# The last store of an AdaLoRA forward kernel: two rows per partition taken out of it and sent in nineteen small transfers

## The chip, the cores and the metric

The kernel runs on one core of a Trainium2 chip. A core has five engines that run at the same time: TensorE (PE) for matrix products, VectorE (DVE), ScalarE (ACT), GpSimd (POOL) and SyncE (SP). Each works through its own list of instructions in order, and they wait for each other by semaphores. Sixteen DMA engines move data between the chip's memory (HBM) and the core's own memory (SBUF, 128 partitions). A transfer is issued by an instruction of one of the engines; from then on the DMA engines do the work, and when it has landed its semaphore has risen by 16.

The metric is the time of one execution on the device in microseconds (us). Lower is better.

## The reference

`x` is 16 x 2048 rows of 256 numbers, all float32, `W` is 256 x 256, `lora_A` is 256 x 16, `lora_B` is 16 x 256, `lora_E` has 16 numbers and `scale` is 1.0.

```python
x_flat = x.reshape(-1, in_dim)                 # 32768 x 256
y = x_flat @ W
lora_out = x_flat @ lora_A
lora_out = lora_out * lora_E
lora_out = lora_out @ lora_B
y = y + scale * lora_out
return y.reshape(batch, seq_len, out_dim).astype(np.float32)
```

33.6 MB of `x` have to come in and 33.6 MB of `y` have to go out.

## The kernel before

The small matrices are folded into one at the start: `weff = W + scale * A * E * B` in bfloat16 (lines 149 to 156 and 224 to 233, and TensorE's lines 277 to 287). After that the kernel is one product of `x` with `weff`.

The 32768 rows are cut into 32 steps of 1024 rows (`S` = 8 rows in each of 128 partitions). Steps are grouped into chunks by `PLAN`: ten chunks of three steps and a last one of two. A chunk is what one load or one store moves: 24 rows of 1 KB per partition, 3 MB, or in the last chunk 16 rows per partition, 2 MB. `rows_of` (line 114) gives a chunk's rows in HBM, and a partition's rows lie there one behind the other; `rows_at` (line 118) gives them in SBUF. The tensor `xy` holds four buffers of 24 rows, and `X_AT` and `Y_AT` say which buffer a chunk of `x` or of `y` uses.

Each step goes through the engines like this. VectorE rounds its rows to bfloat16 (`xb`, line 198). TensorE transposes them (line 258), ScalarE or VectorE copies the transposed rows to `xt` (line 188), which keeps 22 steps, VectorE moves a step to `xm` (line 211), TensorE multiplies it with `weff` in two halves (line 267), and ScalarE or VectorE copies each half from PSUM to the buffer of `y` (line 180). The order of VectorE's work is written out in `VECTOR`, and TensorE's comes from `FIRST` and `SECOND`.

All transfers are issued by SP, in this order: `w_sb`, the first chunk of `x`, `a_sb`, `b_sb`, `e_sb`, the other ten loads, and then the eleven stores. A load whose buffer is in use waits for the transposes that read it (line 128). A store waits until both halves of its last step have been copied (semaphores `s_rdy`, line 140), and the first store also waits for the last load but one (line 143). Loads and stores of chunk `i` share the semaphore `s_io[i]`: 16 once `x` has landed, 32 once `y` has.

After the last store has been issued, SP waits for the first eight stores (line 146), which closes the first block of the program. A second block at the end (lines 298 to 300) waits for the last three stores. It shows in the profile under line 331, where the program is closed.

GpSimd makes the identity matrix and `b_bf`, and then it only passes on semaphores (lines 159 to 164). It issues no transfers.

Of the kernel before, what the change touches and what calls it, by code (L numbers as in the profile page):

```python
# [9 lines left out]
S, Q = 8, 4  # L10

PLAN = [3] * 10 + [2]
# [4 lines left out]
Y_AT = [3, 1, 2, 0, 3, 1, 2, 0, 3, 1, 2]  # L17

KEPT = 22


FIRST = [6, 7, *range(14, 28)]
# [12 lines left out]
def kernel(  # L35
# [10 lines left out]
    nc = tc.nc  # L46
    P = 128
# [4 lines left out]
    out_flat = out.flatten_outer_dims()  # L52
# [4 lines left out]
    H = S // Q  # L57
    CHUNKS, STEPS = len(PLAN), sum(PLAN)
# [4 lines left out]
    def sbuf(name, shape, dt):  # L63
        return ctx.enter_context(nc.sbuf_tensor(name, shape, dt))
# [7 lines left out]

    xt = sbuf("xt", [P, KEPT, S, P, KC], BF16)
    xm = [sbuf(f"xm{s}", [P, S, P, KC], BF16) for s in range(2)]
# [15 lines left out]
    sem = tc.alloc_semaphore  # L90
    s_w = sem("s_w")
    s_l = sem("s_l")
    s_io = [sem(f"s_io{i}") for i in range(CHUNKS)]
    s_id = sem("s_id")
    s_lora = sem("s_lora")
    s_lpe = sem("s_lpe")
# [7 lines left out]
    s_rdy = [sem(f"s_rdy{h}") for h in range(H)]  # L104
# [9 lines left out]
    def rows_of(flat, i):  # L114
        r0, n = first[i] * S * P, PLAN[i] * S
        return flat[r0:r0 + n * P, :].rearrange("(p b) k -> p b k", b=n)

    def rows_at(buffer, r, rows):
        return xy[:, at[buffer] * S + r:at[buffer] * S + r + rows, :]

    with tc.tile_critical(sync_engine=mybir.EngineType.SP, no_gpsimd_drain=True):  # L121
        sp, pe, dve, act, pool = nc.sync, nc.tensor, nc.vector, nc.scalar, nc.gpsimd
# [15 lines left out]
        for i in range(CHUNKS):  # L138
            for h in range(H):
                sp.wait_ge(s_rdy[h], i + 1)  # L140
            if i == 0:

                sp.wait_ge(s_io[CHUNKS - 2], 16)
            sp.dma_start(out=rows_of(out_flat, i), in_=rows_at(Y_AT[i], 0, PLAN[i] * S)).then_inc(s_io[i], 16)
        for i in range(CHUNKS - 3):
            sp.wait_ge(s_io[i], 32)

# [4 lines left out]
            out=ident[:], in_=ident[:], compare_op=mybir.AluOpType.not_equal, fill=1.0,  # L152
# [6 lines left out]
        for k in range(STEPS):  # L159
            pool.wait_ge(s_mv, k + 1).then_inc(s_m, 1)  # L160
            i = chunk[k] - 1
            if k > 0 and i >= 0 and k == first[i + 1]:
                for h in range(H):
                    pool.wait_ge(s_rdy[h], i + 1).then_inc(s_y[h], 1)


        known = {}

        def ensure(engine, semaphore, value):
            if known.get((engine, semaphore.name), 0) < value:  # L170
                engine.wait_ge(semaphore, value)
                known[engine, semaphore.name] = value
# [11 lines left out]
        def transposes_of(k, engine, copy):  # L184
            ensure(engine, s_t, k + 1)
            if k >= KEPT:
                ensure(engine, s_mv, k - KEPT + 1)
            copy(  # L188
                out=xt[:, k % KEPT].rearrange("w j p c -> w j (p c)"), in_=ps_xt[k % 2][:].bitcast(BF16),
            ).then_inc(s_c[k % 2], 1)  # L190
# [11 lines left out]
        def move(k):  # L202
# [6 lines left out]
            if k >= 2:  # L209
                ensure(dve, s_p, (k - 1) * H)  # L210
            dve.tensor_copy(out=xm[k % 2][:], in_=xt[:, k % KEPT]).then_inc(s_mv, 1)  # L211

        vectors = set(VECTOR.split())
        for what in VECTOR.split():
            n = int(what[1:])
# [8 lines left out]
            if what == "r0":  # L224
# [3 lines left out]
                    out=ate[:], in0=ps_at, scalar1=e_sb[:], scalar2=float(scale),  # L228
# [69 lines left out]
    with tc.tile_critical(sync_engine=mybir.EngineType.SP, no_gpsimd_drain=True):  # L298
        for i in range(CHUNKS - 3, CHUNKS):
            nc.sync.wait_ge(s_io[i], 32)  # L300


# [33 lines left out]
```

## Time and profile before

| What | Value |
|---|---|
| time, median of 2 runs | 166.28 us (166.25 to 166.31) |
| time of the profiled execution | 166.21 us |
| its span, from the first to the last instruction | 164.4 us |
| TensorE busy | 103.4 us (63%) |
| VectorE busy | 99.9 us (61%) |
| ScalarE busy | 72.1 us (44%) |
| GpSimd busy | 1.6 us (1%) |
| moved by DMA | 67.43 MB, mean 410 GB/s over the span |
| last store (2 MB), from issue to landing | 13.7 us |

The profile counts times from the first instruction of the span. Its page cuts the span into 40 equal slices, here of 4.1 us, and gives one digit for each: 9 means busy for 90% or more. The row "DMA" is the mean over the 16 DMA engines. In the list of waits each line names the waiting engine and line, what it waited for, the total in us, the number of times, and the longest; a small q behind an engine's name means its sequencer. A line of the timeline has start, duration, engine, source line, operation and the names written and read.

### The profile page before, as it was taken

How to read it: one execution, taken by the hardware profiler on the slowest of the kernel's cores; microseconds unless marked ns; L12 is line 12 of the kernel's file. 1: busy time of each engine (PE TensorE's matmuls, PEld its weight loads, DVE VectorE, ACT ScalarE, POOL GpSimd, SP SyncE). 2: the span in 40 equal slices, each digit the busy share in tenths (PEclk: the TensorE clock that was granted, in tenths of full speed). 3: DMA queues.
4: the chain of work that ended last, by engine and by line, in shares of the span. 5: the costliest groups of instructions: out<-in, count | busy, mean ns of one | idle time of the engine just before them, and what ended most of it. 6: DMA issues, size and time to landing. Idle time of an engine off the chain costs nothing. (4 is left out here: it accounts for less than half of the span.)

```text
span 164.4 us, 2431 instructions
## 1 busy us (share of the span) xinstructions
PE 103.4 (63%) x772; PEld 82.0 (50%) x772; DVE 99.9 (61%) x101; ACT 72.1 (44%) x62; POOL 1.6 (1%) x7
## 2 busy tenths in 40 slices
PE   0003763858884567966799887878878787880000
PEld 0001652747674447745699665655666565560000
DVE  0016699786969496787999765667466466730000
ACT  3000254146796413441477665446546544652000
POOL 1002000000000000000000000000000000000000
PEclk9999999599999675599999999999999999999555
DMA  5999999999999999999999999999999999999970
GB/s 165 460 403 460 401 460 401 460 401 460 401 466 395 466 395 466 395 466 385 420 460 401 454 407 460 413 442 424 436 424 436 424 432 424 442 424 430 426 301 12
DMA packets 3523, 67.43 MB, mean 410 GB/s; under 512 B 560, under 2 KB 576, under 8 KB 704
## 3 DMA queue, kind: packets, MB, share of 16 engines
q1 hardware_dynamic: 3520, 67.41, 96.2%
q14 instruction: 3, 0.02, 0.0%
HBM read 33.85 MB, written 33.55 MB: 410 GB/s over the span
## 5 line engine op out<-in xcount | busy, mean ns | idle before, releaser
L267 PE MATMUL ps_y<-weff,xm 128*128 128x256 bf16 x512 | 62.8, 272 | 9.9 <-PEq L264 8.8
L180 ACT COPY xy<-ps_y 128x1024 f32<-128x1024 f32 x49 | 48.7, 1016 | 35.2 <-PE ps_y L267 34.5
L267 PEld LDWEIGHTS ps_y<-weff,xm 128*128 128x128 bf16 x512 | 47.3, 97 | 24.3 <-issue 19.2
L258 PE MATMUL ps_xt<-ident,xb 128*128 128x128 f32 x256 | 41.4, 319 | 21.9 <-PEq L256 21.8
L198 DVE CAST xb<-xy 128x2048 bf16<-128x2048 f32 x32 | 38.6, 1221 | 23.7 <-DMA xy<-in_x_dram 20.2
L258 PEld LDWEIGHTS ps_xt<-ident,xb 128*128 128x128 f32 x256 | 34.7, 165 | 28.2 <-issue 28.1
L188 ACT COPY xt<-ps_xt 128x2048 bf16<-128x2048 bf16 x12 | 22.4, 1868 | 41.1 <-PE ps_xt L258 41.1
L180 DVE COPY xy<-ps_y 128x1024 f32<-128x1024 f32 x15 | 18.4, 1225 | 17.2 <-PE ps_y L267 17.2
L188 DVE COPY xt<-ps_xt 128x2048 bf16<-128x2048 bf16 x20 | 24.2, 1216 | 1.0 <-PE ps_xt L258 0.9
L211 DVE COPY xm<-xt 128x2048 bf16<-128x2048 bf16 x32 | 21.8, 685 | 4.4 <-PE ps_y L267 4.4
L280 PE MATMUL ps_y<-ident,a_sb 128*16 128x128 f32 x2 | 0.6, 402 | 12.2 <-DMA e_sb<-in_lora_E_dram 12.2
L280 PEld LDWEIGHTS ps_y<-ident,a_sb 128*16 128x16 f32 x2 | 0.1, 94 | 12.2 <-DMA e_sb<-in_lora_E_dram 12.2
L188 ACT ACT_TABLE_LOAD x1 | 1.3, 1283 | 0.9 <-SPq L121 0.9
L233 DVE TENSOR_TENSOR weff<-w_sb,ps_y 128x512 bf16<-128x512 f32 x1 | 0.7, 687 | 0.8 <-PE ps_y L284 0.8
L156 POOL CAST b_bf<-b_sb 16x256 bf16<-16x256 f32 x1 | 0.9, 912 | 10.6 <-DMA e_sb<-in_lora_E_dram 10.6
L284 PE MATMUL ps_y<-b_bf,ate 16*128 16x256 bf16 x2 | 0.6, 404 | 0.6 <-DVE ate L227 0.6
L284 PEld LDWEIGHTS ps_y<-b_bf,ate 16*128 16x128 bf16 x2 | 0.1, 106 | 1.1 <-DVE ate L227 1.1
L227 DVE TENSOR_SCALAR ate<-ps_y,e_sb 16x256 bf16<-16x256 f32 x1 | 0.5, 472 | 0.0
L151 POOL TENSOR_SCALAR_AFFINE_SELECT ident<-ident 128x128 f32<-128x128 f32 x1 | 0.3, 294 | 0.2 <-POOL ident L149 0.2
L149 POOL MEMSET ident<- 128x128 f32 x1 | 0.2, 205 | 0.5 <-SPq L121 0.5
L317 POOL MEMSET const-bfloat16-1.0<- 128x1 bf16 x1 | 0.1, 103 | 0.0
L317 POOL MEMSET const-uint8-127<- 128x1 uint8 x1 | 0.1, 102 | 0.0
(2 smaller groups left out, 0.2 us busy)
## 6 DMA issues: line engine op xcount, KB each, us to landing
xy<-in_x_dram SPq DMA_DIRECT2D x10, 3072.0 KB, 14.4
out_dram<-xy SPq DMA_DIRECT2D x10, 3072.0 KB, 12.5
xy<-in_x_dram SPq DMA_DIRECT2D x1, 2048.0 KB, 12.7
out_dram<-xy SPq DMA_DIRECT2D x1, 2048.0 KB, 13.7
w_sb<-in_W_dram SPq DMA_DIRECT2D x1, 256.0 KB, 2.7
a_sb<-in_lora_A_dram SPq DMA_DIRECT2D x1, 16.0 KB, 9.4
b_sb<-in_lora_B_dram SPq DMA_DIRECT2D x1, 16.0 KB, 9.2
e_sb<-in_lora_E_dram SPq DMA_DIRECT2D x1, 0.1 KB, 9.4
```

What stands on the lines that cost most here:

```text
L151: pool.affine_select(out=ident[:], in_=ident[:], compare_op=mybir.AluOpType.not_equal, fill=1.0, base=0, pattern=[[-1, P]], channel_multip ...
L156: pool.tensor_copy(out=b_bf[:], in_=b_sb[:]).then_inc(s_lora, 1)
L180: done = copy(out=rows_at(Y_AT[i], (k - first[i]) * S + h * Q, Q), in_=ps_y[h][:])
L188: copy(out=xt[:, k % KEPT].rearrange("w j p c -> w j (p c)"), in_=ps_xt[k % 2][:].bitcast(BF16),).then_inc(s_c[k % 2], 1)
L198: dve.tensor_copy(out=xb[k % 2][:], in_=rows_at(X_AT[i], (k - first[i]) * S, S),).then_inc(s_xb, 1)
L211: dve.tensor_copy(out=xm[k % 2][:], in_=xt[:, k % KEPT]).then_inc(s_mv, 1)
L227: dve.tensor_scalar(out=ate[:], in0=ps_at, scalar1=e_sb[:], scalar2=float(scale), op0=mybir.AluOpType.mult, op1=mybir.AluOpType.mult,).the ...
L233: dve.tensor_add(out=weff[:], in0=w_sb[:], in1=ps_aeb).then_inc(s_lora, 1)
L258: t = pe.transpose(ps_xt[b][:, j, :], xb[b][:, j, :].bitcast(FP32), ident[:])
L267: m = pe.matmul(ps_y[h][:, j, :], xm[b][:, h * Q + j, :, c], weff[:, c, :], start=(c == 0), stop=(c == KC - 1),)
L280: t = pe.transpose(ps_at[:, c, :], a_sb[:, c, :], ident[:])
L284: m = pe.matmul(ps_aeb[:, c, :], ate[:, c, :], b_bf[:], start=True, stop=True)
```

## The change

The last store, that of chunk 10, no longer covers all 16 rows of each partition. It moves the first 14, in one transfer as before. Row 15 of the 128 partitions follows in sixteen transfers on SP's queue: the first takes 15 partitions, the next 14, and so on down to 1, and the last takes the remaining 8. Row 14 goes in three transfers that GpSimd issues, of 5, 11 and 112 partitions. GpSimd waits for the same two semaphores as SP's last store before it issues them. Each of the two groups has a semaphore of its own, and the block at the end waits for both, after the large stores. All bytes that were stored before are still stored.

```diff
--- before.py
+++ after.py
@@ -17,6 +17,10 @@
 Y_AT = [3, 1, 2, 0, 3, 1, 2, 0, 3, 1, 2]
 
 KEPT = 22
+
+
+PIECES = [*range(15, 0, -1), 8]
+POOL_PIECES = [5, 11, 112]
 
 
 FIRST = [6, 7, *range(14, 28)]
@@ -91,6 +95,8 @@
     s_w = sem("s_w")
     s_l = sem("s_l")
     s_io = [sem(f"s_io{i}") for i in range(CHUNKS)]
+    s_sp = sem("s_sp")
+    s_po = sem("s_po")
     s_id = sem("s_id")
     s_lora = sem("s_lora")
     s_lpe = sem("s_lpe")
@@ -141,7 +147,20 @@
             if i == 0:
 
                 sp.wait_ge(s_io[CHUNKS - 2], 16)
-            sp.dma_start(out=rows_of(out_flat, i), in_=rows_at(Y_AT[i], 0, PLAN[i] * S)).then_inc(s_io[i], 16)
+            rows = PLAN[i] * S - (2 if i == CHUNKS - 1 else 0)
+            sp.dma_start(out=rows_of(out_flat, i)[:, :rows], in_=rows_at(Y_AT[i], 0, rows)).then_inc(s_io[i], 16)
+
+        def pieces(engine, semaphore, row, sizes):
+            p = 0
+            for n in sizes:
+                engine.dma_start(
+                    out=rows_of(out_flat, CHUNKS - 1)[p:p + n, row:row + 1],
+                    in_=rows_at(Y_AT[-1], row, 1)[p:p + n],
+                ).then_inc(semaphore, 16)
+                p += n
+            assert p == P
+
+        pieces(sp, s_sp, PLAN[-1] * S - 1, PIECES)
         for i in range(CHUNKS - 3):
             sp.wait_ge(s_io[i], 32)
 
@@ -162,6 +181,11 @@
             if k > 0 and i >= 0 and k == first[i + 1]:
                 for h in range(H):
                     pool.wait_ge(s_rdy[h], i + 1).then_inc(s_y[h], 1)
+
+
+        for h in range(H):
+            pool.wait_ge(s_rdy[h], CHUNKS)
+        pieces(pool, s_po, PLAN[-1] * S - 2, POOL_PIECES)
 
 
         known = {}
@@ -298,6 +322,8 @@
     with tc.tile_critical(sync_engine=mybir.EngineType.SP, no_gpsimd_drain=True):
         for i in range(CHUNKS - 3, CHUNKS):
             nc.sync.wait_ge(s_io[i], 32)
+        nc.sync.wait_ge(s_sp, len(PIECES) * 16)
+        nc.sync.wait_ge(s_po, len(POOL_PIECES) * 16)
 
 
 # ---- launch: one core; inputs and outputs as the reference has them ----
```

## The prediction

> **What bounds it now.** I read the page's slices first, then what SyncE (SP) waited for, then short windows at the end of the span.
>
> ```profile
> span 164.4 us, 2431 instructions
> ...
> DMA  5999999999999999999999999999999999999970
> ...
> PE 1%; ACT 1%; issue 0%
> PE ps_y L267 1%; ACT xy L180 1%
> ```
>
> The DMA engines are busy in every slice but the last two, while the chain of compute that ended last is 2% of the span: it stops at 149.2 us with ScalarE's last copy, and the span runs 15.2 us longer. SP's waits say on what (waited for: us in total, times, longest):
>
> ```profile
> SPq L331 <- DMA out_dram<-xy: 12.5, 1, 12.5
> ...
> SPq L143 <- DMA xy<-in_x_dram: 6.9, 1, 6.9
> ```
>
> The 12.5 us is the last store. It is issued at 149.28 and lands 13.7 us later, at 163.0; then come 1.4 us of closing work, and 1.8 us lie outside the span (166.21 - 164.43). Windows of half a microsecond show how the DMA engines run out (last two columns: mean busy share of the 16 engines, GB/s):
>
> ```profile
> 158.50:159.00 0.50, 0.00 (x0) 0.00 (x0) 0.00 (x0) 0.00 (x0) 0.00 (x0) 0.50 0.92 393
> 159.00:159.50 0.50, 0.00 (x0) 0.00 (x0) 0.00 (x0) 0.00 (x0) 0.00 (x0) 0.50 0.24 98
> 159.50:160.00 0.50, 0.00 (x0) 0.00 (x0) 0.00 (x0) 0.00 (x0) 0.00 (x0) 0.50 0.08 33
> ...
> 161.50:162.00 0.50, 0.00 (x0) 0.00 (x0) 0.00 (x0) 0.00 (x0) 0.00 (x0) 0.50 0.08 33
> 162.00:162.50 0.50, 0.00 (x0) 0.00 (x0) 0.00 (x0) 0.00 (x0) 0.00 (x0) 0.50 0.00 0
> ```
>
> 33 GB/s in half a microsecond is 16 KB: one packet of the last store. So after 159.5 hardly more than one packet starts in each window: one engine is late. In the stage where all store, 430 GB/s over 16 engines is 27 GB/s each, so a packet of 16 KB takes 0.61 us, and the last one, begun before 162.0, ends near 162.5. The other engines stop near 159.2. The end of the kernel is therefore the end of **one late engine**, some 3.3 us behind the others. No view names it. An even split gives it 8 of the 128 partitions.
>
> **The change, part by part.**
>
> *The large store loses 2 of 16 rows per partition.* On the late engine that is 8 x 2 KB = 16 KB, 0.61 us at 27 GB/s: **-0.61**.
>
> *What a row of 1 KB costs as a packet of its own.* From below: 1 KB at 27 GB/s, 0.04 us. From above: the load of w_sb, in rows of 2 KB, moved at a mean 289 GB/s from 1.9 to 2.9 us, its slow beginning included; that is 18 GB/s per engine, 0.11 us for a row twice as long. Between them stand the three small loads, queued behind the first load of x on the same queue:
>
> ```profile
> 11.68 1.23 DVE L198 CAST xb<-xy 128x2048 bf16<-128x2048 f32 x1 [11.68 <-DMA xy<-in_x_dram]
> 12.23 0.11 PEld L280 LDWEIGHTS ps_y<-ident,a_sb 128*16 128x16 f32 x2 [12.23 <-DMA e_sb<-in_lora_E_dram]
> ```
>
> x had landed by 11.68 and all three by 12.23: per engine 8 rows of a_sb, one of b_sb, one of e_sb, and three completions, in about 0.55 us, or 0.05 us a packet. I take **0.05** with its completion, as this row is nearest in form. That these are loads and ours are stores is why both ends stay in the range.
>
> *The row over GpSimd's queue* (5, 11 and 112 partitions) is 8 packets on the late engine if the spread is even: **+0.40** (0.32 to 0.88).
>
> *The row in sixteen transfers* of 15 down to 1 and 8 partitions cannot be spread evenly: each has fewer partitions than there are engines. If each puts one partition on each of as many engines, beginning with the same one, the engines receive 16, 15, ... 1, 0 packets. The late engine's part is thus 0 to 16 packets: 0 to +0.80 at 0.05. I take the mean of 8, **+0.40**, for want of a view that names the engine.
>
> *Two more waits of SP after the last one*, each a semaphore instruction like the six of that line (median 28 ns): with their gaps about **+0.1**.
>
> The sum is -0.61 + 0.40 + 0.40 + 0.10 = **+0.3 us**; with none of the sixteen on the late engine it is -0.1, with all sixteen +0.7.
>
> The Trainium skill, "DMA: Bandwidth & Descriptors", section "Latency and other measured facts", says that engines 7 and 15 are usually slower than the rest; and its section on why a DMA increments its semaphore by 16 has a transfer from SP use the lowest-numbered engines. No view here can name an engine; by these rules the sum would be -0.1 for 15 (no packet) and +0.35 for 7 (nine packets), both inside my sum's bounds.
>
> **What hides the rest.** The sixteen issues stand on SP behind the large store. SP's issues at the start show their price (start, us):
>
> ```profile
> 0.95 0.38 SPq L131 DMA_DIRECT2D w_sb<-in_W_dram  x1
> 1.38 0.42 SPq L129 DMA_DIRECT2D xy<-in_x_dram  x1
> ...
> 2.80 0.55 SPq L135 DMA_DIRECT2D e_sb<-in_lora_E_dram  x1
> 3.39 1.42 SPq L129 DMA_DIRECT2D xy<-in_x_dram  x3
> ```
>
> Five issues from 0.95 to 3.39 are 0.49 each, so sixteen take 7.8 us, from 149.7 to 157.5. Behind them on SP stand the waits for the first eight stores, long landed, and the barrier of the block, under a microsecond; the final wait begins near 158.4 instead of 150.6, still ahead of 163.0. The last piece, issued at 157.0, lands by 159.7 if it takes the 2.7 us that w_sb took from issue to landing. The cover is the late engine: 163.0 - 159.7 = 3.3 us. It is gone when an issue costs over 0.49 + 3.3/15 = 0.71 us.
>
> GpSimd waits for the last copies (149.2) and then issues three transfers. It has no DMA in this trace: its instructions take 0.1 to 0.9 us, SP's issues 0.5, so 0.3 to 2.7 us for three; I take 1.5. They are hidden until 163.0 - 2.7 = 160.3, that is up to 3.7 us each. Their packets come ahead of part of SP's backlog, but on an engine that never stops this shifts bytes and adds none.
>
> The fast engines carry at most -0.61 + 0.40 + 0.80 = +0.6 more and end near 159.8: they do not become the bound at 0.05 a packet; at 0.11 (+2.0) they end at 161.2, not either.
>
> **The forecast** stands on the profiled execution, 166.21 us, which lies 0.07 below the median of 166.28: 166.21 + 0.3 = 166.5, or **166.4** with the two ends of the uneven row weighed a little to its lighter side.
>
> **Rivals.**
>
> 1. *The late engine gets none, or nearly none, of the sixteen* (-0.1): 166.1, at the best price 0.04: -0.61 + 0.32 + 0.1 = -0.2, 166.0. For it: one row is dealt out unevenly, and an engine of the thin end gains. Against: nothing shows that the late engine is there. It is one end of the forecast's own case.
> 2. *SP is blocked while many transfers are out*, which is the slower side. Most shown without a stall is seven (x0, a, b, e, x1 to x3 issued by 4.8 us, w_sb landed at 3.65); here there would be up to eighteen. If the eighth has to wait, eleven pieces follow after the store before the last lands (144.40 + 13.7 = 158.1): 158.1 + 11 x 0.49 + 2.7 = 166.2, 3.2 later than 163.0, or about 169.5; after the last store, 163.0 + 8.1, it would be 174. It decides when the last piece cannot be issued before 160.3.
> 3. *GpSimd's first transfers are dear*: at 5 us each they land at 149.2 + 15 + 2.7 = 166.9, giving about 170. For it: no row shows one. Against: 11 us of cover.
> 4. *A queue of GpSimd costs a fixed time at the program's start or end*, where nothing covers it: priced by the 1.4 us of closing work and the 1.8 outside, +0.5 to +3: 167 to 169.5.
> 5. *The large store no longer goes in one run per partition*: 14 rows of 1 KB as 112 packets on the late engine, 5.6 us instead of 4.25: 167.7.
> 6. *The small transfers pay a fixed time each, one after another*: at w_sb's 2.7 us from issue to landing, sixteen take 43 us and the store stage ends near 193, which would give 196. Against: the three small loads passed in 0.55 us together. This is what the Trainium skill's advice would make of it (same page, "Rules for kernel authors": many small transfers are better made one, since under 64 KB one pays mostly overhead); the trace of the three loads speaks against it.
>
> Faster by over 2% (about what a measurement of this kernel can tell from no change; 3.3 us) would need the late engine's whole lag to vanish. The change takes 0.61 from it and gives at least 0.3 back.
>
> **Chances.** The forecast's case, rival 1 in it: 0.73 (rival 1 alone 0.35). Rival 2: 0.07. Rival 3: 0.05. Rival 4: 0.08, a quarter of it over 2%. Rival 5: 0.04. Rival 6: 0.01. Faster by over 2%: 0.02. Slower by over 2%: 0.07 + 0.05 + 0.02 + 0.01 = 0.15, and the rest, 0.83, within 2%. The range reaches from rival 1 at the low price less 0.1 for the measurement, 165.9, to all sixteen packets on the late engine at 0.11 (24 x 0.11 - 0.61 + 0.1 = +2.1), 168.3; rival 5 and the smaller half of rival 4 lie in it, rivals 2, 3 and 6 outside.
>
> **What would show it.** The landing of the last store before 163.0 and the tail of half-microsecond windows with one late engine still in it, moved by under 0.7 us, bear the sum out. SP's sixteen issues over more than 11 us, with a gap among them, would be rival 2; GpSimd's DMAs last to land, rival 3; an equal last landing with a longer span or more time outside it, rival 4; more than 128 packets of the large store, rival 5. The forecast is wrong if the last wait of SP ends on a piece and not on the large store.

## The result and the profile after

The changed kernel takes 168.92 us (168.86 to 168.97, 2 runs) where the kernel before took 166.28 (166.25 to 166.31). The ratio is 1.0159, with a 95% interval of 1.0142 to 1.0176: 2.6 us slower. The forecast was 166.4, with a range of 165.9 to 168.3, so the result lies above the range.

The page of the changed kernel, in the lines that answer to those shown of before (the span, the DMA row of the 40 slices, the queues, of which q0 carries GpSimd's transfers, and the chain that ended last):

```profile
span 167.1 us, 2452 instructions
...
DMA  5999999999999999999999999999999999999920
...
q1 hardware_dynamic: 3776, 67.27, 94.5%
q0 software_dynamic: 112, 0.13, 0.2%
...
POOL out_dram L156 1%; PE ps_y L291 1%; ACT xy L204 1%; POOLq L187 0%
```

The span is 2.7 us longer and the time outside it is the same, 1.8 us, so the loss is inside. The chain now ends on GpSimd (POOL). Whoever stops reading here blames GpSimd's transfers; the experiments show that this is wrong. SP's waits (in total, times, longest) point elsewhere:

```profile
SPq L357 <- DMA out_dram<-xy: 3.3, 2, 2.1
```

Two waits at the end make up the 3.3 us. The last block's waits run in the order GpSimd's pieces, SP's pieces, large stores, the reverse of the order in the source. The first lasts 1.2 us, until 163.4, and the second, for SP's own pieces, lasts 2.1 us more, until 165.6. What moved in that time (half-microsecond windows; mean busy share of the DMA engines and GB/s at the end of the line):

```profile
162.50:163.00 0.50, 0.00 (x0) 0.00 (x0) 0.00 (x0) 0.00 (x0) 0.00 (x0) 0.50 0.07 21
163.00:163.50 0.50, 0.00 (x0) 0.00 (x0) 0.00 (x0) 0.00 (x0) 0.00 (x0) 0.50 0.03 8
163.50:164.00 0.50, 0.00 (x0) 0.00 (x0) 0.00 (x0) 0.00 (x0) 0.00 (x0) 0.50 0.00 0
164.00:164.50 0.50, 0.00 (x0) 0.00 (x0) 0.00 (x0) 0.00 (x0) 0.00 (x0) 0.50 0.00 0
164.50:165.00 0.50, 0.00 (x0) 0.00 (x0) 0.00 (x0) 0.00 (x0) 0.00 (x0) 0.50 0.00 0
165.00:165.50 0.50, 0.00 (x0) 0.00 (x0) 0.00 (x0) 0.00 (x0) 0.00 (x0) 0.50 0.00 0
```

**Nothing moved.** No packet starts after 163.5, and SP still waits for two microseconds. What comes in that time are completions. The trace records each increment of a semaphore by a DMA engine; these are the last twelve of the semaphore of SP's pieces, in us:

```
163.22 163.61 163.80 163.99 164.19 164.38 164.58 164.77 164.96 165.16 165.35 165.55
```

They come 0.194 us apart, one after another; the first gap is twice as long, and GpSimd's last increment falls into it, at 163.41. The large store's last increment, at 163.02, is the one ahead of them; it came as before (162.99). The twelve packets that these completions belong to had gone out at 0.048 us each (0.042 for the row and 0.006 for the 4-byte packet of its completion), the last by 163.2. So the data costs what the forecast put, and the completions cost four times as much.

On the two profiled executions the whole loss is 168.86 - 166.21 = 2.65 us. Of it 0.03 is the later landing of the large store, 2.53 lies between that landing and the last one (thirteen times 0.194), and 0.09 comes after it, where two more waits stand.

### The profile page after: what moved, and what is told of

Same layout as the page of the kernel before. It is cut to its first block, busy times and chain, and to the rows that moved or that the text cites. A ratio compares the mean times of both kernels' runs of the same rounds, so it can differ in the third digit from the quotient of the medians.

```text
span 167.1 us, 2452 instructions
## 1 busy us (share of the span) xinstructions
PE 107.1 (64%) x772; PEld 85.9 (51%) x772; DVE 100.0 (60%) x101; ACT 72.1 (43%) x62; POOL 3.4 (2%) x10
## 5 line engine op out<-in xcount | busy, mean ns | idle before, releaser
L282 PE MATMUL ps_xt<-ident,xb 128*128 128x128 f32 x256 | 45.1, 340 | 18.2 <-PEq L280 18.1
L282 PEld LDWEIGHTS ps_xt<-ident,xb 128*128 128x128 f32 x256 | 38.5, 179 | 24.4 <-issue 24.3
L156 POOL DMA_DIRECT2D out_dram<-xy x3 | 1.7, 583 | 142.6 <-issue 142.6
```

The costliest lines, as they stand in the source:

```text
L156: engine.dma_start(out=rows_of(out_flat, CHUNKS - 1)[p:p + n, row:row + 1], in_=rows_at(Y_AT[-1], row, 1)[p:p + n],).then_inc(semaphore, 16)
L282: t = pe.transpose(ps_xt[b][:, j, :], xb[b][:, j, :].bitcast(FP32), ident[:])
```

## The experiments

Three theories stood against each other. The **completion theory**: on the late DMA engine the completions of small stores are settled one after another, 0.19 us each, and twelve of the sixteen transfers use that engine. The **issue theory**: SP's sixteen issues took long, from 149.94 to 161.34 instead of the 7.8 us forecast, and the last piece comes late. The **GpSimd theory**: its transfers, the first of them issued 6.4 us after its wait had passed, are the cause, as the chain says.

### The two parts alone

Each of these runs does one part of the change; the other row goes back into the large store.

```diff
-            rows = PLAN[i] * S - (2 if i == CHUNKS - 1 else 0)
+            rows = PLAN[i] * S - (1 if i == CHUNKS - 1 else 0)
...
-        pieces(pool, s_po, PLAN[-1] * S - 2, POOL_PIECES)
```

> Row 14 goes back into the large store; the sixteen transfers on SP's queue stay, nothing is issued by GpSimd. Completion theory (on the late DMA engine the small transfers' completions are settled one after another, 0.19 us each, twelve of them): nearly all of the loss stays, +2.0 to +2.8 us against the kernel before, with a row of landings 0.19 us apart at the end. Issue theory (SP took 11.4 us for its sixteen issues instead of 7.8, because the engines were busy, and the last piece comes late): also +2 to +2.8, with the issues as long as before. GpSimd theory (its late and slow transfers hold up the others, SP's issues too): -0.5 to +0.5, and SP's issues take 0.5 us each.

Measured: 168.73 us against 166.33, ratio 1.0142 (1.0125 to 1.0159). Nearly all of the loss is here, without GpSimd. Twelve increments run from 163.25 to 165.48, 0.19 to 0.25 us apart. SP's issues are as slow as in the changed kernel:

```profile
149.82 0.33 SPq L149 DMA_DIRECT2D out_dram<-xy  x1
150.20 11.45 SPq L154 DMA_DIRECT2D out_dram<-xy  x16
```

So the slow issues are not GpSimd's doing either.

```diff
-        pieces(sp, s_sp, PLAN[-1] * S - 1, PIECES)
...
-        pieces(pool, s_po, PLAN[-1] * S - 2, POOL_PIECES)
+        pieces(pool, s_po, PLAN[-1] * S - 1, POOL_PIECES)
```

> Row 15 goes in GpSimd's three transfers of 5, 11 and 112 partitions, row 14 goes back into the large store, SP issues no small transfer. Completion theory: three small completions on the late engine at most, -0.3 to +0.6 us against the kernel before. Issue theory: -0.3 to +0.3. GpSimd theory: +2 us or more. In all three the first of GpSimd's transfers should again be issued some 6 us after its wait has passed, if that is the cost of its first use.

Measured: 166.64 us against 166.33, ratio 1.0021 (1.0011 to 1.0030), 0.3 us slower. GpSimd's transfers start late again:

```profile
149.24 0.33 SPq L149 DMA_DIRECT2D out_dram<-xy  x1
155.18 1.73 POOL L154 DMA_DIRECT2D out_dram<-xy  x3 [142.04 <-issue]
```

The last of them lands at 163.54, 0.2 us behind the large store, which itself lands at 163.36 here. The GpSimd theory falls: its part of the loss is about 0.3 us, and one completion behind the large store's makes up 0.2 of that.

### The same bytes in one, eight and sixteen transfers

In these runs row 15 goes over SP's queue in another cut, and GpSimd sends nothing.

```diff
-PIECES = [*range(15, 0, -1), 8]
+PIECES = [128]        # e3
+PIECES = [16] * 8     # e5
+PIECES = [8] * 16     # e4
```

> Row 15 goes in one transfer of 128 partitions on SP's queue: the same bytes and, on an even spread, eight packets of 1 KB on each engine, but one completion each. No transfer of GpSimd. Completion theory: -0.3 (the row out of the large store) + 0.4 (eight packets) + 0.2 (one completion) = +0.3 us, between 0 and +0.6. If it were the rows of 1 KB that cost 0.19 us each and not the transfers: 8 x 0.19 - 0.3 = +1.2. Issue theory: about 0.

Measured: 166.48 against 166.33, ratio 1.0007 (0.9998 to 1.0017), 0.15 us. The bytes in rows of 1 KB cost next to nothing; it is not the rows.

> Row 15 goes in eight transfers of 16 partitions on SP's queue, row 14 in the large store, nothing from GpSimd. Completion theory: each engine, the late one too, gets eight, so eight landings 0.19 us apart behind the large store's: 8 x 0.19 + about 0.1 = +1.4 to +1.8 us against the kernel before, wherever the late engine stands. Issue theory: eight issues at 1.2 us end near 160 instead of 161.3, so at most +1.

Measured: 168.00 against 166.35, ratio 1.0095 (1.0080 to 1.0110), 1.65 us. Eight increments from 163.17 to 164.53, each 0.194 us after the one before. The last issue ends at 158.9, 4 us before the large store lands, so the issue theory has nothing here to explain the loss with. Every DMA engine has the same eight rows to move in this run and in the one before it; what is new is seven more completions on each, and the time is 1.5 us longer.

> Row 15 goes in sixteen transfers of 8 partitions each on SP's queue, no transfer of GpSimd. Issue theory: sixteen issues as in the changed kernel, +2 to +2.8 us. Completion theory: what counts is how many of them sit on the late engine. If a transfer of 8 uses the first eight engines and the late one is among them (the twelve landings point to the fifth), all sixteen do: 16 x 0.19 + 0.5 - 0.3 = about +3.2, with sixteen landings 0.19 us apart; if the late engine is among the other eight, none: about -0.3.

Measured: 169.43 against 166.33, ratio 1.0190 (1.0173 to 1.0207), 3.1 us. All sixteen sit on the late engine: the increments end at 166.12, the last twelve of them 0.194 us apart. With so many the data is held up as well: the first fourteen packets on that engine take 0.046 us each, the last two 0.156 and 0.194.

### Which engine is the late one

Twelve of the sixteen transfers of the change use the late engine. If a transfer of n partitions uses the first n engines, twelve of the list (15 to 5, and 8) reach the fifth engine. This can be tested by transfers that just miss it and just reach it. The first try took the pieces from part of the partitions and cut the large store to fit:

```diff
+            cuts = [(0, P, rows)] if i < CHUNKS - 1 else [(64, P, rows), (0, 64, rows - 1)]
+            for p, q, n in cuts:
+                sp.dma_start(
+                    out=rows_of(out_flat, i)[p:q, :n], in_=rows_at(Y_AT[i], 0, n)[p:q],
+                ).then_inc(s_io[i], 16)
...
+PIECES = [4] * 16     # e6; in e7 the cut is at 80 and PIECES is [5] * 16
```

> Sixteen transfers of 4 partitions on SP's queue carry row 15 of partitions 0 to 63; row 15 of the others stays in the large store, which goes in two transfers (64 partitions of 16 rows, 64 of 15). Completion theory, with the late engine the fifth: none of the sixteen uses it, so only the second half's completion is new there, -0.1 to +0.4 us. If the late engine were one of the first four: +3. Issue theory: seventeen issues as slow as before, +2 to +3.

> As the run with transfers of 4 partitions, but the sixteen take 5 partitions each (partitions 0 to 79; the large store in 48 partitions of 16 rows and 80 of 15). Completion theory, with the late engine the fifth: all sixteen sit on it, +2.8 to +3.6 us with sixteen landings 0.19 us apart. If the late engine is the sixth to the eighth: about 0, as with 4. Issue theory: +2 to +3.5 in both runs.

Measured: 171.21 us with transfers of 4 (ratio 1.0277, 1.0259 to 1.0295) and 171.04 with 5 (1.0288, 1.0256 to 1.0321). Both lie above every expectation, because the cut of the large store has a price of its own, and so they do not test the completion theory. The run with transfers of 4:

```profile
154.00:158.00 4.00, 0.00 (x0) 0.00 (x0) 0.00 (x0) 0.00 (x0) 0.00 (x0) 0.50 1.00 256
158.00:162.00 4.00, 0.00 (x0) 0.00 (x0) 0.00 (x0) 0.00 (x0) 0.00 (x0) 0.50 1.00 253
```

The kernel before in the same place:

```profile
154.00:158.00 4.00, 0.00 (x0) 0.00 (x0) 0.00 (x0) 0.00 (x0) 0.00 (x0) 0.50 0.99 422
```

With every engine busy, the two halves of 64 partitions move at 255 GB/s instead of 422. The large store lands at 164.67 with transfers of 4 and at 163.99 with 5, and SP's issues take longer still, up to 2.2 and 3.3 us each. These are the lines of the run with 4 and then of the run with 5:

```profile
152.16 14.97 SPq L158 DMA_DIRECT2D out_dram<-xy  x16
```

```profile
151.62 14.46 SPq L158 DMA_DIRECT2D out_dram<-xy  x16
```

The issues end at 167.13 and 166.08, behind the large store's landing, the last piece lands about 1 us after that, and in neither run does SP's list of waits show a wait for a store at the end. So in these two SP's issues come last, as the issue theory has it. In the change they do not: SP stands at its final waits from 162.24 on, and the large store lands at 163.02.

The second try leaves the large store in its 128 partitions and puts the partitions that are left over into one more small transfer:

```diff
-PIECES = [*range(15, 0, -1), 8]
+PIECES = [64] + [4] * 16     # e9
+PIECES = [48] + [5] * 16     # e10
```

> The large store is whole again in its 128 partitions, less row 15. Row 15 goes in one transfer of 64 partitions and sixteen of 4, all on SP's queue. Completion theory with the late engine the fifth: only the first of the seventeen uses it, so one landing behind the large store's, -0.3 + 0.2 + 0.2 + 0.1 = +0.2 us (0 to +0.5). If the late engine is one of the first four, +3.3. Issue theory: seventeen issues, +2.5 to +3.0; with 1.2 us an issue until 158.4 and 0.34 after, the last one stands at 161.8 and lands at 162.8, just before the large store.

> The same with one transfer of 48 partitions and sixteen of 5: the number of issues is the same, the bytes are the same, each small transfer has one partition more. Completion theory with the late engine the fifth: seventeen completions sit on it, 17 x 0.19 - 0.3 + 0.4 = +3.2 to +3.6 us, with seventeen landings 0.19 us apart. If it is not among the first five: as with 4. Issue theory: as with 4.

Measured: 167.01 us with transfers of 4 (ratio 1.0045, 1.0029 to 1.0060) and 170.22 with 5 (1.0231, 1.0216 to 1.0247), against 166.30. **One partition more per transfer costs 3.2 us.** The issues are the same in number and time; these are the lines of the run with 4 and then of the run with 5:

```profile
150.05 12.01 SPq L154 DMA_DIRECT2D out_dram<-xy  x17
```

```profile
150.04 11.77 SPq L154 DMA_DIRECT2D out_dram<-xy  x17
```

and SP's wait for the stores at the end is 0.2 us with 4 partitions and 3.7 with 5:

```profile
SPq L351 <- DMA out_dram<-xy: 0.2, 1, 0.2
```

```profile
SPq L351 <- DMA out_dram<-xy: 3.7, 1, 3.7
```

With 5, the increments after the large store's landing run on to 166.46. This settles the place of the cost, the fifth engine in the order in which transfers fill them, and the issue theory falls as the cause of the loss in the change.

It keeps a smaller part. With transfers of 4 the loss of 0.7 us is above the expected 0 to 0.5. There SP reaches its final wait only at 163.02, when the large store has landed already (162.83); and in the closing work SP stands still for 0.4 us, which the runs with sixteen issues behind an uncut large store do not show. The run with 5 has the same standstill, so about 3.5 of its 3.9 us are the completions and their packets. What the standstill is was not tested.

What the seven runs with an uncut large store and SP's pieces behind it give together, in us (the count on the late engine follows from the first-n order; SP's pieces only):

| PIECES | on the late engine | large store lands | last piece lands | between | ratio |
|---|---|---|---|---|---|
| [128] | 1 | 163.02 | 163.33 | 0.31 | 1.0007 |
| [64] + [4] * 16 | 1 | 162.83 | 163.23 | 0.40 | 1.0045 |
| [16] * 8 | 8 | 162.99 | 164.53 | 1.54 | 1.0095 |
| 15 to 1, 8 | 12 | 163.07 | 165.48 | 2.41 | 1.0142 |
| 15 to 1, 8, and GpSimd's (the change) | 12 | 163.02 | 165.55 | 2.53 | 1.0159 |
| [8] * 16 | 16 | 162.92 | 166.12 | 3.20 | 1.0190 |
| [48] + [5] * 16 | 17 | 163.07 | 166.46 | 3.39 | 1.0231 |

From eight pieces on, the time between the landings is 0.19 to 0.20 us for each (in the change thirteen share it, with GpSimd's last). With one, the 0.31 us are mostly the eight rows themselves, which go out 0.042 us apart. In the second row the last landing may be that of another engine, because SP's last issue ends only at 162.06.

Why the fifth engine is late is not shown. In the kernel before an engine falls behind store by store: the last of a store's sixteen increments comes 0.2 us after the fifteenth at the third store, and 2.4 us after it at the ninth.

### Small transfers ahead of the large store

If only the settling is slow and data can go on meanwhile, small transfers cost nothing where more data stands behind them. This run is made from the kernel before.

```diff
+PIECES = [32] * 4
...
+            if i == CHUNKS - 1:
+                pieces(sp, s_sp, PLAN[-1] * S - 1, PIECES)
+            rows = PLAN[i] * S - (1 if i == CHUNKS - 1 else 0)
```

> Row 15 goes in four transfers of 32 partitions, two packets on each engine, and SP issues them ahead of the large store instead of behind it. Behind it, by the runs with one and eight transfers, four would cost about +0.8 us. Completion theory: the late engine still has store 9 to move when they are queued and the large store behind them, so the four settle while data moves: -0.3 + 0.4 + 0.1 = +0.1 to +0.3. If each completion stops the engine's data too, +0.8 as behind. If SP's issue of the large store, 5 us later, is what counts: the fast engines idle from 154.5 on, and the end moves only if the late engine idles too, which it does not before 157.7.

Measured: 166.43 against 166.30, ratio 1.0008 (0.9999 to 1.0017). On the late engine the four increments come at 158.47, 158.67, 158.87 and 159.07, again 0.2 us apart, while the large store's data goes on behind them; it lands at 163.15. So four with data behind them cost nothing. More than four were not tried there, and the run with sixteen transfers of 8 shows that many unsettled completions do hold up packets behind them.

### A lighter load for the late engine

An attempt at a version faster than both:

```diff
-            sp.dma_start(out=rows_of(out_flat, i), in_=rows_at(Y_AT[i], 0, PLAN[i] * S)).then_inc(s_io[i], 16)
+            cuts = [(0, P)] if i < CHUNKS - 1 else [(16, P)] + [(p, p + 4) for p in range(0, 16, 4)]
+            for p, q in cuts:
+                sp.dma_start(
+                    out=rows_of(out_flat, i)[p:q], in_=rows_at(Y_AT[i], 0, PLAN[i] * S)[p:q],
+                ).then_inc(s_io[i], 16)
```

> From the kernel before: the last store goes in one transfer of 112 partitions (seven packets of 16 KB on each engine instead of eight) and four transfers of 4 partitions (one packet of 16 KB each on the first four engines), no row of 1 KB. If the late engine is the fifth, it has 16 KB less and no small completion: -0.6 us (-0.4%), the first four engines end near 161, still ahead of it. If the late engine is one of the first four: +1.8 + 4 x 0.19 = about +2.5. Issue theory: four more issues, hidden, 0.

Measured: 167.74 against 166.35, ratio 1.0079 (1.0058 to 1.0099): slower by 1.4 us where 0.6 faster was expected. As in the two runs with a cut store, the engines are busy and move less, here 375 GB/s between 154 and 158 us against 422. Why another division of the partitions is slower was not tried. None of the kernels beats the kernel before.

### GpSimd's first transfer

```diff
-        sp.dma_start(out=b_sb[:], in_=lora_B).then_inc(s_l, 16)
+        pool.dma_start(out=b_sb[:], in_=lora_B).then_inc(s_b, 16)
```

> As the run with GpSimd's three transfers alone, but GpSimd also issues the load of b_sb at the start instead of SP. If the 6 us before GpSimd's first transfer are paid once, at its first use, the three at the end are issued within 0.5 us of 149.3 and 6 us are seen at the start; if they belong to the busy DMA engines or to that place of the program, the three are late again. The time: between -0.3 and +0.6 us against the kernel before, the end is the large store's in both.

Measured: 166.47 against 166.30, ratio 1.0010 (1.0000 to 1.0020). GpSimd's timeline:

```profile
1.48 0.64 POOL L165 DMA_DIRECT2D b_sb<-in_lora_B_dram  x1 [1.04 <-SPq L126]
...
149.60 1.58 POOL L154 DMA_DIRECT2D out_dram<-xy  x3 [136.55 <-ACT xy L203]
```

With a transfer early in the program, the three at the end go out at once. The delay belongs to the first use, but neither theory of it is quite right: at the start that first use costs 0.5 us (GpSimd's first instruction there stands at 0.95 without it, and this one at 1.48), not 6. Why it costs 6 at the end stays open.

## Why the prediction was wrong

**What bounds the kernel** was right: the end is that of one late DMA engine. It stayed so in every run but three: the two with a cut large store, where SP's issues came last, and the one with the lighter load, where the large store moved at 375 GB/s.

**The step that failed is the price of a row as a packet of its own, "0.05 with its completion".** On the DMA engine's queue that was right: a row and the packet of its completion take 0.048 us. But SP waits for the increments, and those of one engine come 0.194 us apart, in series, so SP's last long wait ended on a piece, which the prediction itself had named as the sign that it is wrong. The term for the row in sixteen transfers is 12 x 0.194 = 2.33 us on the late engine, instead of 0.40; in the run with this part alone the last piece landed 2.41 us behind the large store.

The three small loads had not shown otherwise; they were divided by the wrong count. Their 0.55 us hold ten packets but also three completions, and 0.55 / 3 is 0.18 us for each. The trace of the kernel before bears out the second reading: the last packet of the three loads starts at 11.38 us, and the increments run on from the last one of x, at 11.66, to 12.19. So the small loads took about 0.18 us for each completion, if the last three stand on one engine, close to the 0.194 of the stores. I had kept 0.11 as the upper end, taken from the bytes of another load; no end of the range held a price per transfer.

**The other terms.** -0.61 for the large store and +0.40 for GpSimd's row were to give -0.21 together. Measured are +0.03 in the landing of the large store and one completion of GpSimd's behind it, 0.19. The 0.61 us were not won back on the clock: the large store's last packet ended 0.2 us earlier, with GpSimd's packets taken in between, and its landing came 0.7 us after that instead of 0.5, behind another increment of GpSimd's at 162.82. The two waits cost 0.09 where 0.1 was put. With 2.33 in place of 0.40 the forecast's sum gives +2.2, against 2.65 measured.

**What was luck.** The prediction gave 0.83 to a time within 2% of the kernel before, and 1.6% came out. That was the count of twelve, not the sum: with seventeen completions on the late engine it was 2.3%.

**The engine's place** had been left open between 0 and 16 packets, with a mean of 8; it got 12. (The sixteen counts have no 8 among them: nine transfers reach the eighth engine and seven the ninth.) The Trainium skill's rule in "DMA: Bandwidth & Descriptors" (its section on why a DMA increments its semaphore by 16) that SP's transfers use the lowest-numbered engines agrees with these runs: 4 partitions miss the late engine and 5 reach it. The Trainium skill's remark on the same page that engines 7 and 15 are usually slower (section "Latency and other measured facts") names, as a guess at the cause, transfers issued from GpSimd. The kernel before has none, so the remark had little to say here: the late engine is the fifth, in every run that tells.

**SP's issues** were mis-sized, and it was hidden as far as the change goes. They took 1.2 us each while the engines still had the large stores to move, and 0.34 after 158.4:

```profile
149.94 8.40 SPq L156 DMA_DIRECT2D out_dram<-xy  x7
```

```profile
158.38 2.95 SPq L156 DMA_DIRECT2D out_dram<-xy  x9
```

The first line is the window up to 158.38 in the changed kernel, the second the window from there. At the start five issues took 0.49 each, and the three loads behind them 0.47 each with 3 MB and more queued ahead, so a full queue alone does not make an issue slow; what does is not shown. Rival 2, SP blocked while many transfers are out, was right in kind; its point of decision, the last issue at 160.3, was passed (161.3) and yet it did not decide, since the fast engines' pieces landed by 162.7, within 1.4 us of their issue and not 2.7.

**Rival 3 and rival 4** (GpSimd's first transfer dear, or a fixed time for its queue): the first use did cost 6 us, more than I had thought of, and the cover of 11 us held but for about 0.3 us. The time outside the span did not change. **Rival 5**: the large store went in packets of 14 KB, one per partition; it didn't come.

**Rival 6**, a fixed time for each small transfer, one after another, was the right mechanism, and I gave it one chance in a hundred at a price fourteen times too high (2.7 us). I had refuted it with the three loads, which do refute 2.7 us each, but not 0.18. The Trainium skill's advice named beside it, to make many small transfers into one, is what the run with one transfer bears out: 0.15 us for the same bytes. The Trainium skill's same page also says, of transfers issued from GpSimd ("Anatomy of one DMA — SWDGE (gpsimd) path"), that a semaphore's update waits until the last byte is confirmed in memory. That would fit the 0.5 us between the end of the large store's last packet and its landing in the kernel before. That completions queue at 0.19 us each, and so lag by up to 2.4 us, is shown by these runs alone; why it is 0.19 stays open.

## What to carry to other kernels

Count the transfers that stand last on the DMA engine that ends last, not the bytes: as stores at the end of the kernel they cost 0.19 us each, while the same bytes in one transfer cost 0.15 us in all, and four of them with data behind them nothing that could be measured. When a wait at the end goes on in windows where no data moves, look at the increments of its semaphore one by one, and at what was waited for last; the chain of work had named the wrong engine here. And when a price is read from a stretch of the trace, divide it by each thing that it holds: 0.55 us over its packets gave 0.05, over its three completions 0.18, and the second was near the truth.

## What the runs showed of the hardware that I had not expected

- Completions of small stores on one engine are settled 0.194 us apart, though their packets follow each other in 0.048 us. Four of them did not hold up the data behind them (166.43 us against 166.30); of sixteen, the last two packets took 0.156 and 0.194 us instead of 0.046.
- The large store in its 128 partitions moves at 422 GB/s; cut into two transfers of 64 partitions it moves at 255, and 112 partitions with four transfers of 4 behind at 375, with all engines shown as busy.
- SP's first issue behind a large store took 0.33 us (0.56 in one run), and the next ones about 1.2 us each as long as uncut large stores were being moved, however few partitions they had (1.24 for 128 and 1.3 for 15). In the run with four transfers ahead of the large store the four took 0.33, 1.18, 1.20 and 1.51.
- GpSimd's first transfer of a program stood 6 us behind its wait at the end of the kernel and 0.5 us at its start.
